# Writing the value projections and the fills of a context stage behind the small work of its pair

## The chip, the cores and the metric

The kernel runs on one NeuronCore of a Trainium2 chip. Its engines run side by side, each through its own queue in a fixed order: PE (TensorE) multiplies matrices, DVE (VectorE), ACT (ScalarE) and POOL (GpSimd) work on elements, and SP (SyncE) here only issues DMAs. The metric is the device time of one execution in microseconds. A profile of one execution gives each instruction's start and length; its times count from the start of the span.

## What is computed

Two layers of a backbone over 512 latent tokens and 256 context tokens, model width 1024, batch 1, all in float32. Layer 0, in which the change lies, is bidirectional RWKV-7 time mixing beside a gated short convolution; layer 1, a convolution module, isn't touched. What matters of layer 0:

```python
def wkv_scan(S0, r, decay, k, v, kk, a, reverse):
    def step(S, inp):
        r_t, w_t, k_t, v_t, kk_t, a_t = inp
        sa = jnp.einsum("bhvk,bhk->bhv", S, -kk_t)
        S = (S * w_t[:, :, None, :]
             + sa[..., None] * (kk_t * a_t)[:, :, None, :]
             + v_t[..., None] * k_t[:, :, None, :])
        return S, jnp.einsum("bhvk,bhk->bhv", S, r_t)
    ...
    rc, kc, vc, zac, bc, cc, xc, zbc = jnp.split(hc @ w_in, EVEN_SPLITS, axis=-1)
    yac, S_f, S_b = rwkv_seq(rwkv_prep(hc, rc, kc, vc, *rw), zero, zero, r_k, lnx_w, lnx_b, ctx_out)
    r, k, v, za, bg, cg, xb, zb = jnp.split(h @ w_in, EVEN_SPLITS, axis=-1)
    ya, _, _ = rwkv_seq(rwkv_prep(h, r, k, v, *rw), S_f, S_b, r_k, lnx_w, lnx_b, True)
    yb = bg * dwconv(cg * xb, sc_w, seg_len)
    y = jnp.concatenate([ya.astype(h.dtype) * jax.nn.silu(za), yb * jax.nn.silu(zb)], axis=-1) @ w_out
```

The scan runs over the context first, in both directions, and its end states start the scan over the latents. Of the context only these states are needed.

## The kernel before

The 16 heads lie in 8 pairs of 128 channels (0 to 7). The scan is done in chunks of 64 tokens: what happens within a chunk is matrix work that doesn't depend on the state ("small work"), and a "chain" carries the state from chunk to chunk. There are 12 stages. Stages 0 to 3 are context stages; one takes two head pairs together, with 4 chunks in each direction, and its state has a name c0 to c3. Stages 4 to 11 are latent stages l0 to l7, one head pair with 8 chunks each. So c2 holds the head pairs 4 and 5.

What a stage needs, and the helpers that write it:

- `project(p, which)` computes r, k or v (0, 1, 2) of head pair p: a weight block is loaded by SP in two halves (`wr`), ACT casts each to a high part (`wh`, L128), DVE subtracts the low part (`wl`, L129), and 24 matmuls (three products for each of 8 blocks of the contraction) go into `pl` for the 512 latent columns, for context stages 24 more into `pc` for 256 context columns. `shifted` mixes neighbouring tokens: one ACT pass (L370) and two DVE passes (L371, L373). The latent result goes to DRAM (`psp`) through POOL's queue.
- `prep_ctx(b)` projects k and v of both head pairs of a context stage. `prep_lat(p)` only loads k, v and r of a latent stage back.
- `fills(x)` holds the projections that a later stage needs: r of pair p when `FILL_R[p]` is x, and the gate z (`gate`, tile `pza`) when `FILL_Z[p]` is x. So `fills(1)` is z1 to z3, `fills(2)` r2, `fills(3)` r3 and z4 to z7, `fills(4)` r4 to r7. `conv_branch(p)` has four projections (`pcg`, `pxb`, `pbg`, `pzb`); branch 0 is written at the end of stage 3.
- `light` makes decays and scaled keys from k (tiles `ss`, `lw`, `la` on PE, then `AR`, `BK`). `heavy` does the products within chunks by a string of letters (`HEAVY`): V `pv`, the centred v copied into `UV` by four ACT copies (L640); B `pb`, transposes of keys into `BKt`; A `pa`, the products that are masked into `E` (in context stages `ectx`, L610); N copies of blocks of `E` into `Nt`; O the latent bonus.
- `solve` inverts small triangular blocks: a DVE transpose (L661) and 62 short DVE steps (L667, L669). `merge` completes the inverse (L675 to L694; its 64 matmuls go into `uh1`).
- `chain_ctx` and `chain_lat` are the chains (`zoc`, `zol`, `uh0`). A step goes PE, ACT, PE, ACT, PE, DVE; matmuls of the chains are pinned in the written order.

The main loop writes, in stage s, the chain of s, and then what the string `STAGE` says: O the bonus, F `fills(s + 1)`, P the preparation of stage s + 2, L and H light and heavy work of stage s + 2, S and M solve and merge of stage s + 1, C a conv branch. What is written earlier has the higher priority. A scheduler then fixes one order for each engine: it takes, by its own estimate of times, the ready instruction with the highest priority. So a letter's place in the string doesn't say where an instruction ends up, only what it yields to. The estimate ends there: on the chip each engine runs through its queue in that order.

Buffers also tie the parts: `k_`, `v_` and `Y` have one buffer each, `cg` and `yb` take turns for the latent results on their way to DRAM.

## Time and profile before

| | us |
|---|---|
| median of three runs | 1439.53 |
| lowest and highest of them | 1431.3, 1440.98 |
| the profiled execution | 1434.6 |
| its span, from the first to the last instruction | 1432.5 |

A line of a table of stretches gives the stretch, its length, the busy time of each engine with the number of instructions, and then the granted TensorE clock (1.00 is full speed), the busy share of the DMA engines and what they moved. PEld is the loading of weights into PE, beside its matmuls. A float32 matmul shows as two records, a transpose or one of the projections' as one. Matmuls are pipelined, and their ends are modelled, so that a PE which counts as busy isn't always at its peak. In the chain of work that ended last each row is a piece of time on the path to the end.

### The profile page before, as it was taken

Reading aid. Unit: us, or ns where it says so; the run is one execution under the profiler, and the core shown is the slowest. Engines: PE = TensorE matmul, PEld = TensorE weight load, DVE = VectorE, ACT = ScalarE, POOL = GpSimd, SP = SyncE. Lnnn points to the kernel's source line nnn. Section 1 sums busy time; section 2 is a strip of 40 time slices with the busy share of each in tenths; the row PEclk is TensorE's granted clock in tenths of the full one; section 3 lists DMA queues with packets and bytes.
Section 4 is the critical chain, followed back from the end, with each engine's and each line's share of the span. In section 5 each row is a group of like instructions: output and inputs, shape, how many; then the busy total and the mean of one; then the engine's idle time right before and its main releaser. Section 6 shows DMA issues by size and latency. Waiting matters only on the chain.

```text
span 1432.5 us, 29756 instructions
## 1 busy us (share of the span) xinstructions
PE 1376.7 (96%) x11921; PEld 1008.3 (70%) x11921; DVE 983.0 (69%) x2294; ACT 749.5 (52%) x1516; POOL 117.9 (8%) x246
## 2 busy tenths in 40 slices
PE   6899999999998998999999999999999999999998
PEld 1464677878776766666666666778777777788886
DVE  2675597568678989999999999656745545544333
ACT  4636355254555666756667565456753423464322
POOL 2023210000101101011010100010000000000000
PEclk9999999979898999999999999999999999999999
DMA  9754433222322221222222312358813303133322
GB/s 322 226 177 161 156 111 97 92 60 61 93 87 75 82 81 60 77 75 71 83 77 68 98 43 92 110 174 321 265 45 118 119 9 109 59 100 92 103 89 88
DMA packets 137626, 158.54 MB, mean 111 GB/s; under 512 B 15375, under 2 KB 104143, under 8 KB 137369
## 3 DMA queue, kind: packets, MB, share of 16 engines
q1 hardware_dynamic: 121104, 106.47, 23.7%
q0 software_dynamic: 15312, 48.99, 10.5%
q8 instruction: 94, 1.54, 0.4%
q10 hardware_dynamic: 1072, 1.19, 0.2%
q14 instruction: 44, 0.36, 0.1%
HBM read 138.33 MB, written 18.28 MB: 109 GB/s over the span
## 4 chain that ended last, share of the span: by engine, by line
PE 63%; DVE 14%; ACT 5%; issue 2%; DMA 0%; DVEq 0%; ACTq 0%
PE pu L57 12%; PE pz L57 6%; PE f L57 6%; PE o L57 5%; PE uh L57 4%; PE zol L57 4%; PE pcg L57 3%; PE pxb L57 3%; PE pza L57 3%; DVE E L610 2%; PE plk L57 2%; PE zoc L57 2%; PE pzb L57 2%; PE plv L57 1%; PE pac L57 1%
## 5 line engine op out<-in xcount | busy, mean ns | idle before, releaser
L57 PE MATMUL o<-wh,y 128*128 128x512 f32 x248 | 79.6, 397 | 0.0
L667 DVE TENSOR_TENSOR xtmpl<-Xl,Yl 128x126 f32<-128x126 f32 (+22 forms) x248 | 62.3, 251 | 2.8
L669 DVE TENSOR_TENSOR Yl<-Yl,xtmpl 128x126 f32<-128x126 f32 (+22 forms) x248 | 62.3, 251 | 2.7
L1152 ACT CAST ah<-a 64x512 fp32r<-64x512 f32 x32 | 19.8, 619 | 72.2 <-DVE a L1147 71.8
L57 PE MATMUL pal<-ARl,BKl 64*128 64x128 f32 x512 | 46.3, 300 | 10.7 <-DVE E L610 4.9
L57 PE MATMUL zol<-UV,E 64*64 64x64 f32 (+1 forms) x1024 | 54.2, 221 | 0.0
L57 PEld LDWEIGHTS o<-wh,y 128*128 128x128 f32 x248 | 45.9, 188 | 9.5
L57 PEld LDWEIGHTS pal<-ARl,BKl 64*128 64x128 f32 x512 | 36.4, 194 | 22.2 <-issue 7.2
L57 PE MATMUL zol<-Hl,ARl 64*64 64x64 f32 x896 | 50.2, 230 | 1.2 <-DVE Hl L782 1.0
L775 ACT COPY UV<-uh 64x128 f32<-64x128 f32 x128 | 33.2, 260 | 33.1 <-PE uh L57 25.6
L57 PE MATMUL o<-wl,y 128*128 128x512 f32 x124 | 49.4, 398 | 1.2 <-DVE wl L129 1.2
L57 PEld LDWEIGHTS zol<-Hl,ARl 64*64 64x64 f32 x896 | 35.0, 133 | 21.2 <-issue 17.0
L129 DVE TENSOR_TENSOR wl<-wr,wh 128x1024 fp32r<-128x1024 f32 x28 | 34.2, 1222 | 19.7 <-ACT wh L128 17.0
L57 PEld LDWEIGHTS uh<-UV,BKt 128*64 128x64 f32 x704 | 26.3, 137 | 28.7 <-ACT UV L775 23.0
L1147 DVE TENSOR_TENSOR a<-pu,a 128x512 f32<-128x512 f32 x16 | 11.0, 690 | 50.5 <-PE pu L57 48.2
L57 PEld LDWEIGHTS zol<-UV,E 64*64 64x64 f32 (+1 forms) x1024 | 42.4, 136 | 2.8 <-ACT UV L775 2.1
L610 DVE TENSOR_TENSOR E<-pal,maskE 128x512 f32<-128x512 f32 x64 | 42.9, 685 | 2.0 <-PE pal L57 1.2
L1107 DVE SCALAR_TENSOR_TENSOR pr<-px,dbe,What 119x512 f32<-119x512 f32 x32 | 22.6, 746 | 26.8 <-PE px L57 26.8
L782 DVE SCALAR_TENSOR_TENSOR Hl<-uh,PCl,HPl 128x64 f32<-128x64 f32 x112 | 26.5, 277 | 19.5 <-PE uh L57 8.6
L128 ACT CAST wh<-wr 128x1024 fp32r<-128x1024 f32 x28 | 29.6, 1056 | 19.7 <-DMA wr<-in_ev_w_out_dram 10.3
L886 POOL DMA_DIRECT2D mwr<-in_mod_w_dram x56 | 29.8, 537 | 112.8 <-PE uh L57 67.7
L57 PE MATMUL uh<-UV,BKt 128*64 128x64 f32 x704 | 36.3, 232 | 2.5 <-ACT UV L775 2.5
(947 smaller groups left out, 4230.9 us busy)
## 6 DMA issues: line engine op xcount, KB each, us to landing
mwr<-in_mod_w_dram POOLq DMA_DIRECT2D x56, 256.0 KB, 3.5
wr<-in_ev_w_out_dram SPq DMA_DIRECT2D x28, 512.0 KB, 5.1
ectx<-in_mod_w_dram SPq DMA_DIRECT2D x12, 512.0 KB, 5.2
wrk<-in_ev_w_in_dram SPq DMA_DIRECT2D x16, 256.0 KB, 3.1
wrv<-in_ev_w_in_dram SPq DMA_DIRECT2D x16, 256.0 KB, 4.1
wrr<-in_ev_w_in_dram SPq DMA_DIRECT2D x16, 256.0 KB, 2.7
wrza<-in_ev_w_in_dram SPq DMA_DIRECT2D x16, 256.0 KB, 2.8
wrcg<-in_ev_w_in_dram SPq DMA_DIRECT2D x16, 256.0 KB, 2.8
```

The costliest lines, as they stand in the source:

```text
L57: return T.matmul(o, lhsT, rhs, start=start, stop=stop)
L128: S.copy(hi, raw)
L129: env["lo"].tensor_tensor(out=lo, in0=raw, in1=hi, op=ALU.subtract)
L610: st["ev"].append(V.tensor_tensor(out=E[:, h, z * NLAT + c0 : z * NLAT + c0 + m, :], in0=pas[h], in1=maskE[:, z * (1 + h) : z * (1 + h) + ...
L667: V.tensor_tensor(out=tv, in0=X[:, :i, i : i + 1].to_broadcast([P, i, m]), in1=Y[:, i : i + 1, c0:].to_broadcast([P, i, m]), op=ALU.mult)
L669: V.tensor_tensor(out=Y[:, :i, c0:], in0=Y[:, :i, c0:], in1=tv, op=ALU.add)
L775: u_ = S.copy(UV[ZR[1 - h], i : 2 * nch - i : 2 * nch - 1 - 2 * i, ZR[h]], uh[ZR[1 - h], 0:2, :])
L782: h_ = V.scalar_tensor_tensor(out=Hn[:, z, :], in0=uh[:, 2 + z, :], scalar=PC[z][:, i : i + 1], in1=HP[:, z, :], op0=ALU.mult, op1=ALU.add)
L886: nc.gpsimd.dma_start(mws[q], I["mod_w"][layer, kt * P : (kt + 1) * P, c0 : c0 + 512])
L1107: V.scalar_tensor_tensor(out=pr[s][:NPROD], in0=px[s][:NPROD], scalar=dbe[:, 0:1], in1=What[:, n * 512 : n * 512 + 512], op0=ALU.add, op1= ...
L1147: V.tensor_tensor(out=a, in0=pp[1], in1=a, op=ALU.mult)
L1152: S.copy(ahl[s][hr], a[hr])
```

## The change

The string for the context stages is split in two. In stages 0 and 1 it becomes `KLSMHVvF`: K projects the keys of stage s + 2, then light, solve, merge and heavy work, then V projects the values, small v does `pv`, and the fills come last. In stages 2 and 3, where no values are projected, it becomes `OPLSMHF`: the fills stand last there too. The string of the latent stages stays. In `heavy` the context string loses V, and the O that did nothing there. `pv` and the bonus look up v when they run. For c0 and c1, ahead of the loop, k and v are still projected together, and `pv` is written behind `heavy`. The switch for a higher priority of weight splits (`env["first"]`) is False throughout.

```diff
-HEAVY = ("VBOAN", "ANBV")
-STAGE = ("OFPLSMH", "OSPLMHFC")
+HEAVY = ("BAN", "ANBV")
+STAGE = ("KLSMHVvF", "OPLSMHF", "OSPLMHFC")
...
-    env = {"lo": V}
+    env = {"lo": V, "first": False}
...
-        return hilo(src, raw, hi, lo)
+        with tc.high_priority() if env["first"] else nullcontext():
+            return hilo(src, raw, hi, lo)
...
-    def prep_ctx(b, between=None):
-        st = state(False, b)
-        for which in (1, 2):
+    def prep_ctx(b, between=None, st=None, kinds=(1, 2)):
+        st = st or state(False, b)
+        for which in kinds:
...
-        v_ = st["v"]
...
-            pv = ch3(ps_at(f"pv{nm}"))
+            pv, v_ = ch3(ps_at(f"pv{nm}")), st["v"]
...
-        st["po"] = po
+        st["po"], st["pv"] = po, pv
...
     heavy(sts[0])
+    sts[0]["pv"]()
...
     heavy(sts[1])
+    sts[1]["pv"]()
...
-        for x in STAGE[s >= 4]:
+        env["first"] = False
+        for x in STAGE[(s >= 2) + (s >= 4)]:
...
+            elif x == "K":
+                sts.append(prep_ctx(s + 2, kinds=(1,)))
+            elif x == "V":
+                prep_ctx(s + 2, st=sts[s + 2], kinds=(2,))
+            elif x == "v":
+                sts[s + 2]["pv"]()
...
-                sts.append(prep_ctx(s + 2) if s < 2 else prep_lat(s - 2))
+                sts.append(prep_lat(s - 2))
```

What the scheduler makes of it is seen at three places. Names carry the stage and a buffer number, and lines from 355 on have moved by one or more in the new file. First, ACT within the light work of c2, where the second half (`ac21`, `iPc21`) follows the first. Before:

```order
L527 ACTIVATE Pc20_2594<-Pc20_2594 128x528
L560 COPY BKc20_2607<-BKc20_2607 64x8x64
L529 COPY PCc20_2599<-Pc20_2594 128x8
L640 COPY UV000_1044<-pvc2_2786 64x8x64 x4
L520 ACTIVATE ac21_2621<-lac21_2618,hcol_77 128x256 x2
L526 ACTIVATE iPc21_2626<-Pc21_2624 128x512
```

Now:

```order
L528 ACTIVATE Pc20_2330<-Pc20_2330 128x528
L371 ACTIVATE vc2_2606<-pcv4_2619,omu_99 128x256
L530 COPY PCc20_2335<-Pc20_2330 128x8
L561 COPY BKc20_2343<-BKc20_2343 64x8x64
L128 CAST whv51_2684<-wrv51_2683 128x512
L521 ACTIVATE ac21_2357<-lac21_2354,hcol_77 128x256 x2
L527 ACTIVATE iPc21_2362<-Pc21_2360 128x512
```

The four copies of V have left this place; an evacuation of the value projection of pair 4 and a cast of the weights for pair 5 have come in.

Second, PE around `pv` of c2. Before, within the light work of c2 (`lac21`), between matmuls of the fill r2:

```order
L57 MATMUL lac21_2618<-lorc_488,lwc2h0_2549 128x256
L57 MATMUL plr2_3076<-hlh_117,whr20_3065 128x512
L57 MATMUL plr2_3076<-hll_118,whr20_3065 128x512
L57 MATMUL plr2_3076<-hlh_117,wlr20_3066 128x512
L57 MATMUL pvc2_2786<-ctr_106,vc2_2407 64x64 x16
L57 MATMUL plr2_3076<-hlh_117,whr20_3065 128x512
```

Now, behind the last mask products of c2 and 23 matmuls of the value projection of pair 5, with the fills z1 to z3 after it:

```order
L57 MATMUL plv5_2717<-hlh_117,whv51_2684 128x512
L57 MATMUL plv5_2717<-hll_118,whv51_2684 128x512
L57 MATMUL plv5_2717<-hlh_117,wlv51_2685 128x512
L57 MATMUL pvc2_2747<-ctr_106,vc2_2606 64x64 x16
L57 MATMUL pza1_2780<-hlh_117,whza10_2769 128x512
L57 MATMUL pza1_2780<-hll_118,whza10_2769 128x512
```

The values' projections now stand within the small work of c2, and the fills alone behind it, ahead of chain c1.

Third, PE at the first light matmuls of l0 (`ssl0`, `lwl00`). Before, behind the last fill z7 and ahead of chain c3:

```order
L57 MATMUL pza7_4081<-hll_118,whza71_4076 128x512
L57 MATMUL pza7_4081<-hlh_117,wlza71_4077 128x512
L57 MATMUL ssl0_4129<-sql0_4127,blk_105 128x512
L57 MATMUL lwl00_4150<-tanhl0_113,lwhl0_4123 128x512
L57 MATMUL lwl00_4150<-tanhl0_113,lwll0_4124 128x512
L57 MATMUL zoc3_0_4471<-UV010_1737,ectx_121 64x64 x8
L57 MATMUL plr4_4658<-hlh_117,whr40_4647 128x512
```

Now, inside chain c2, ahead of its second step:

```order
L57 MATMUL plr3_4276<-hlh_117,whr30_4265 128x512
L57 MATMUL plr3_4276<-hll_118,whr30_4265 128x512
L57 MATMUL ssl0_3923<-sql0_3921,blk_105 128x512
L57 MATMUL lwl00_3944<-tanhl0_113,lwhl0_3917 128x512
L57 MATMUL zoc2_1_3770<-Hc2_0_3731,ARc21_2372 64x64 x2
L57 MATMUL zoc2_1_3770<-Hc2_0_3731,ARc20_2342 64x64 x2
L57 MATMUL zoc2_1_3770<-Hc2_0_3731,ARc21_2372 64x64 x2
```

The light work of l0 has moved one chain ahead; z4 to z7, which stood before it, now stand behind it.

## The prediction

> **What bounds the kernel now.** I read the page first, then a table of stretches, then the chain of work that ended last. The page:

> ```profile
> span 1432.5 us, 29756 instructions
> PE 1376.7 (96%) x11921; PEld 1008.3 (70%) x11921; DVE 983.0 (69%) x2294; ACT 749.5 (52%) x1516; POOL 117.9 (8%) x246
> ...
> PE   6899999999998998999999999999999999999998
> ...
> DVE  2675597568678989999999999656745545544333
> ...
> PEclk9999999979898999999999999999999999999999
> ```

> PE is busy nearly everywhere, so time can only come out of stretches where it waits or runs at a lowered clock. The clock dips (slices 9, 11 and 13) all lie in the context stages. I cut these by the first matmul of each part (columns: stretch, length, then busy us of PE, PEld, DVE, ACT, POOL, then granted clock, DMA share, GB/s):

> ```profile
> core 0: us, PE busy (x) PEld busy (x) DVE busy (x) ACT busy (x) POOL busy (x), PEclk, DMA share, GB/s
> 191.90:225.90 34.00, 33.68 (x355) 24.57 (x355) 27.44 (x62) 22.49 (x44) 2.70 (x5) 1.00 0.32 95
> 225.90:253.30 27.40, 27.40 (x306) 20.48 (x307) 22.39 (x71) 13.83 (x35) 1.62 (x3) 1.00 0.27 82
> 253.30:287.00 33.70, 33.70 (x193) 29.68 (x193) 17.58 (x41) 10.15 (x18) 2.16 (x4) 1.00 0.30 95
> 287.00:320.90 33.90, 30.52 (x351) 24.26 (x350) 23.42 (x44) 19.89 (x40) 1.62 (x3) 0.79 0.21 63
> 320.90:346.10 25.20, 25.20 (x287) 19.89 (x286) 19.07 (x62) 13.82 (x35) 0.55 (x1) 0.95 0.15 44
> 346.10:363.30 17.20, 17.16 (x98) 14.91 (x97) 12.79 (x39) 4.62 (x8) 1.08 (x2) 1.00 0.28 86
> 363.30:396.20 32.90, 30.99 (x349) 23.31 (x347) 24.15 (x45) 20.53 (x41) 5.66 (x10) 0.83 0.31 90
> 396.20:425.00 28.80, 28.80 (x288) 21.75 (x289) 22.62 (x70) 15.78 (x39) 1.62 (x3) 0.96 0.28 80
> 425.00:457.00 32.00, 27.21 (x263) 20.53 (x263) 30.17 (x71) 16.74 (x29) 5.66 (x10) 0.83 0.31 98
> 457.00:484.10 27.10, 26.13 (x348) 19.19 (x345) 21.48 (x66) 18.66 (x45) 1.20 (x3) 0.95 0.20 62
> 484.10:520.50 36.40, 34.01 (x315) 26.15 (x313) 35.20 (x82) 21.88 (x37) 4.59 (x8) 1.00 0.31 91
> 520.50:919.50 399.00, 381.37 (x5315) 269.43 (x5315) 361.19 (x1053) 250.92 (x601) 38.95 (x70) 1.00 0.24 71
> ```

> From the top: small work of pair c1; chain c0; keys and values of c2 alone; small work of c2; chain c1; values of c3 alone; small work of c3; chain c2; small work of latent pair l0; chain c3; small work of l1 with conv branch 0; the latent stages. The waiting is in the small work of c2, c3 and l0 (clock 0.79, 0.83, 0.83), while 33.7 and 17.2 us go to projections that cover nothing. The chain that ended last, in the projections and in the small work of c2 (start, length, what):

> ```profile
> 261.88 2.88 PE pck L57 x24
> 264.75 5.56 PE plk L57 x24
> ...
> 287.23 0.86 PE ssc L57 x2
> ...
> 296.58 0.48 ACT UV L640
> 297.08 0.58 ACT UV L640
> 297.67 0.58 ACT UV L640
> 298.26 0.58 ACT UV L640
> 298.87 0.84 ACT ac L520 x2
> ...
> 301.28 0.69 DVE ARc L551
> ...
> 306.67 1.92 PE uh L57 x64
> 308.58 3.61 PE pac L57 x32
> ...
> 316.31 3.60 PE pac L57 x30
> ```

> The path goes through the four copies of V (L640), which stand on ACT ahead of the second half of the light work, and then through `pac`, 3.60 us for 30 records. In the small work of c1 the same 30 take 2.00 us (timeline rows; the second is pv):

> ```profile
> 219.49 2.00 PE L57 MATMUL pac<-ARc,BKc 64*128 64x64 f32 x30
> ...
> 294.35 1.15 PE L57 MATMUL pvc<-ctr,vc 64*64 64x64 f32 x32
> ```

> **Prices.** A projection is 24 matmuls: 5.56 us over the latent columns, 2.88 over the context ones. So k or v of a context pair is 16.9, a fill 5.56, conv branch 0 22.2. Taking off each stretch the projections that the order puts in it leaves the rest:

> - a chain: c0 27.4 - 16.7 (z1 to z3) = 10.7; c1 25.2 - 14.6 (k7 and nearly all of k6) = 10.6; c2 28.8 - 18.3 (79 matmuls of z4 to z7) = 10.5. I use 10.6.
> - small work: c1 34.0 - 15.5 (67 matmuls) = 18.5; c2 33.9 - 7.9 (r2, 19 context matmuls of k6) = 26.0; c3 32.9 - 9.5 (r3, 17 of z4) = 23.4; l0 32.0 - 12.0 (r4, r5, 4 of r6) = 20.0; l1 36.4 - 22.2 = 14.2.

> So c2 waits some 7.5 us, c3 5, l0 6; all that cover could win is about 18 us. Other prices, groups of the context stages:

> ```profile
> L640 ACT COPY UV<-pvc 64x512 f32<-64x512 f32 x4 | 2.3, 580 | 0.0
> ...
> L128 ACT CAST whk<-wrk 128x512 fp32r<-128x512 f32 x3 | 1.9, 623 | 2.1 <-PE plv L57 2.1
> ...
> L520 ACT ACTIVATE ac<-lac,hcol 128x256 f32<-128x256 f32 x4 | 1.7, 470 | 0.6 <-PE lwc L57 0.6
> ...
> L669 DVE TENSOR_TENSOR Yc<-Yc,xtmpc 128x126 f32<-128x126 f32 (+22 forms) x93 | 23.7, 254 | 2.4
> ...
> L610 DVE TENSOR_TENSOR E<-pal,maskE 128x512 f32<-128x512 f32 x16 | 10.6, 684 | 1.2 <-PE pal L57 1.2
> ...
> L373 DVE SCALAR_TENSOR_TENSOR lr<-plr,hmu,lr 128x511 f32<-128x511 f32 x6 | 4.4, 741 | 0.1
> ...
> wrv<-in_ev_w_in_dram SPq DMA_DIRECT2D x16, 256.0 KB, 4.1
> ```

> **The change, part by part.** No arithmetic is added or removed; every term is an instruction that stands elsewhere. From the end of the small work of c1 (225.9) to the first latent chain (520.5) the kernel takes 294.6 us now. In the new order:

> 1. Chain c0 is covered by k4, k5 in place of z1 to z3: 10.7 + 16.9 = 27.6.
> 2. Small work of c2 holds v4, v5 up to the first matmul of the last one (11.6 us of projections, not 7.9). On the path, the copies of V go (-2.3), but the first evacuation of v (a 128x256 pass of ACT, as L520's: 0.47) and one cast (0.62) come in: -1.2. The extra shifts on DVE fall into its waits (23.4 busy of 33.9). 33.9 - 1.2 = 32.7. Bounds: 18.5 + 11.6 = 30.1 if it runs as c1's did, 26.0 + 11.6 = 37.6 if the larger cover only adds.
> 3. Behind it, uncovered: the other 23 matmuls (5.3), pv (1.15), z1 to z3 (16.7): 23.1. DVE meanwhile solves c2.
> 4. Chain c1 with k6, k7: 27.5.
> 5. Small work of c3: 32.9 - 1.2 = 31.7 (30.1 to 35.0).
> 6. Uncovered: 5.3 + 1.15 + r2 5.56 = 12.0.
> 7. Chain c2 with the light work of l0 inside it, the rest of l0, merge of c3, r3 and z4 to z7. PE: 10.6 + 16.0 (14.2 as in l1, second transpose and pv 1.8) + 27.8 = 54.4. DVE: 22.6 + 30.2 now, 26 solve steps of c3 fewer (-6.6), 34 of l0 more (+8.6), one evacuation pair fewer (-1.5), two masks and a bonus more (+2.1): 55.4. Neither fits beside the other without loss; the latent stages, with the same mix, run DVE at 361.2 of 399.0 (0.905): 55.4 / 0.905 = 61.2. Bounds: 55.4, and one after the other 10.6 + 20.0 + 4.1 (what l0's stretch now leaves to the next: masks' matmuls, transposes, pv) + 27.8 = 62.5.
> 8. Chain c3, l1, r4 to r7, conv branch 0. PE 10.6 + 1.0 + 16.0 + 44.4 = 72.0, of which the last 26.4 us are projections alone; the 45.6 before at the latent stages' PE share (381.4 of 399.0): 47.7. 74.1 (72.0 to 76).

> Sum 289.9, 4.7 less than now. One transpose and pv of l1 (1.8) now stand after 520.5 and are done earlier in the new order: -6.5. The latent stages' own strings are unchanged, so I cost them at nothing; the cover there is the same work in nearly the same order.

> Queues: the weight loads move with their projections on SP. The second half of v5 is loaded behind the two stores of the chain's state, as that of k5 is now; it has 18 us until PE wants it, against 4.1 for a load and 1.3 for cast and difference. On POOL the spills of v stand behind the load of the unit matrix, which waits for the merge; their buffers are written next 20 us later. Both cost nothing, hidden by that work; if the cover failed, 4.1 each.

> The profiled execution took 1434.6 us (span 1432.5); the three runs beside it have the median 1439.5, 0.3% above. Against its own time: 1434.6 - 6.5 = **1428 us**. Why so little: DVE and PE are near full together from 396 on, and the new order leaves 22.0, 10.9 and 26.4 us of projections that cover nothing (parts 3, 6, 8), where now 33.7 and 17.2 stand.

> **Rivals.**

> B, the cover brings the clock back. For it: c1's small work, with 15.5 us of projections in it, shows 1.00 and `pac` at 2.00. Against it: in the new order merge and `pac` still follow each other with six projection matmuls between, as now. Every low bound at once: 27.6 + 30.1 + 23.1 + 27.5 + 30.1 + 12.0 + 55.4 + 72.0 = 277.8, so 294.6 - 277.8 + 1.8 = 18.6 less: 1416 us. [...]

> C, DVE's queue becomes the bound: it is in order, and the values' shifts and the pulled-in solve steps now stand between the light work, the masks and the chain's state updates. For it: 35.2 of 36.4 in l1's stretch. Against it: 23.4 of 33.9 in c2's. Every high bound: 27.6 + 37.6 + 23.1 + 27.5 + 35.0 + 12.0 + 62.5 + 76 = 301.3, 6.7 - 1.8 more: 1439.5, slower than now. It decides from DVE shares above 0.9 in the small work of c2 and c3 on.

> That the change does nothing is excluded by the order: the three places shown all differ.

> **How the numbers follow.** Forecast 0.55, B 0.23, C 0.22. The range goes from B's end, less 2, to C's end plus 6.5 (the span from this execution to the slowest of the runs): 1414 to 1446. About 1% is what a measurement of this kernel tells from no change. Faster by more (below 1420): B's 0.23 and 0.04 of the forecast, 0.27. Slower by more (above 1449): 0.09, the part of C in which the latent stages inherit the delay. Within: 0.64.

> **What would show it.** Each step has its stretch: the small work of c2 and c3 near 32.7 and 31.7 us with L640 gone from the chain; granted clock there still near 0.8 (1.00 with 2.00 us for `pac` would be B); the first light matmul of l0 inside chain c2; DVE above 0.9 from there to chain c3 and idle beside conv branch 0; the first latent chain some 5 us earlier. Wrong would be: PE waiting for projections' casts inside the chains, or DVE above 0.9 in c2's small work (C).

## The result, and the profile after

| | before | after |
|---|---|---|
| median of 6 runs, us | 1438.55 (1431.3 to 1440.98) | 1424.16 (1421.41 to 1426.41) |
| ratio, 95% interval | | 0.991 (0.9892 to 0.9927) |
| the profiled execution, us | 1434.6 | 1423.9 |
| its span, us | 1432.5 | 1421.6 |
| PE busy in it, us | 1376.7 | 1366.3 |
| rest of the span (PE not busy), us | 55.8 | 55.3 |

The forecast was 1428, so the time is 4 us below it and the sign is right. The forecast took 6.5 us off the execution of 1434.6; the spans of the two profiled executions differ by 10.9 us, and the means of all runs (in the table of the experiments) by 12.5. The reason is mostly another one. From the page of the changed kernel:

```profile
span 1421.6 us, 29736 instructions
...
PE 1366.3 (96%) x11921; PEld 999.9 (70%) x11921; DVE 981.5 (69%) x2294; ACT 748.4 (53%) x1516; POOL 118.0 (8%) x246
...
PE   6999998999989998999999999999999999999998
...
PEclk9999998999999999999999999999999999999999
```

PE runs the same 11921 matmuls, and it waits as long as before (55.3 us against 55.8). What became shorter is the matmuls themselves: 10.4 of the 10.9 us of the span are PE's busy time. PE has 23.9 us less of half clock (below), and a microsecond of that costs 0.37 to 0.44 us by the runs further down, which makes 9 to 10.5 us: they come from the clock. The stretches of the changed kernel, cut as in the prediction (same columns; the first row is the small work of c1, then follow the parts 1 to 8 of the prediction, last the latent stages):

```profile
194.30:229.10 34.80, 32.73 (x314) 24.49 (x312) 24.64 (x52) 18.87 (x38) 2.71 (x5) 0.95 0.30 92
229.10:263.00 33.90, 32.20 (x372) 25.64 (x372) 26.27 (x83) 17.69 (x43) 1.09 (x2) 0.90 0.15 46
263.00:289.50 26.50, 25.40 (x320) 20.36 (x319) 24.79 (x57) 18.28 (x37) 1.62 (x3) 1.00 0.24 73
289.50:312.60 23.10, 23.10 (x129) 18.68 (x131) 19.99 (x55) 10.94 (x18) 1.62 (x3) 1.00 0.35 107
312.60:341.10 28.50, 27.83 (x333) 22.58 (x334) 14.60 (x49) 12.90 (x35) 1.08 (x2) 1.00 0.22 65
341.10:367.60 26.50, 25.46 (x321) 20.43 (x320) 23.93 (x47) 18.31 (x37) 5.15 (x9) 1.00 0.28 86
367.60:379.70 12.10, 12.10 (x81) 9.60 (x81) 9.68 (x25) 7.41 (x13) 1.08 (x2) 1.00 0.33 100
379.70:438.00 58.30, 53.39 (x649) 40.57 (x650) 55.84 (x155) 36.74 (x76) 6.79 (x12) 1.00 0.30 90
438.00:509.70 71.70, 69.33 (x700) 53.36 (x694) 55.17 (x126) 42.50 (x87) 7.41 (x14) 1.00 0.34 100
509.70:909.90 400.20, 384.06 (x5286) 270.86 (x5286) 360.84 (x1053) 245.27 (x593) 38.97 (x70) 0.99 0.24 71
```

The small work of c2 and of c3 takes 26.5 us at clock 1.00, where it took 33.9 at 0.79 and 32.9 at 0.83. On the other side, chain c0 (33.9 against 27.4 before) became longer, at 0.90, and the small work of c1 a little (34.8 against 34.0): places where the prediction saw no harm. What lies ahead of c1 ended at 194.3 instead of 191.9; over all profiles of this study that moment lies between 191.9 and 198.7, whatever the kernel.

The profile records when the granted clock changes. In these records it is either full or half (1.00 or 0.50), and each stretch of half clock lasts one to five times 3.41 us (3.4 to 17.1 us in the rows below). Cut along those records, before (ahead of the first, one window of full clock; then the small work of c2, of c3, of l0):

```profile
302.90:306.30 3.40, 1.22 (x18) 0.87 (x18) 3.40 (x6) 3.07 (x6) 0.54 (x1) 1.00 0.00 0
306.30:323.40 17.10, 16.73 (x221) 15.40 (x222) 7.15 (x12) 4.96 (x10) 0.54 (x1) 0.50 0.21 63
384.80:398.50 13.70, 13.70 (x145) 11.59 (x144) 5.72 (x9) 3.45 (x8) 0.55 (x1) 0.50 0.26 79
446.30:459.90 13.60, 13.14 (x184) 10.06 (x183) 9.67 (x16) 4.54 (x9) 1.63 (x3) 0.50 0.30 98
```

With one window of 3.4 us at the start (50.3 us), that is 47.8 us of half clock. (A last stretch, which runs into the end of the span, is left out here and below.) After, all of it (the start; c1; chain c0; the first latent stage):

```profile
48.00:54.80 6.80, 6.16 (x24) 5.50 (x25) 6.70 (x20) 6.80 (x13) 0.00 (x0) 0.50 0.95 292
225.50:232.30 6.80, 6.80 (x81) 6.03 (x80) 1.98 (x3) 2.37 (x4) 0.00 (x0) 0.50 0.08 25
239.10:242.50 3.40, 3.40 (x26) 2.42 (x26) 3.06 (x14) 1.35 (x5) 0.48 (x1) 0.50 0.20 77
549.70:556.60 6.90, 6.56 (x40) 5.09 (x41) 6.54 (x28) 2.58 (x5) 0.00 (x0) 0.51 0.27 78
```

23.9 us, so half of it went: the long stretches in c2, c3 and l0 are gone, and new short ones came in c1, in chain c0 and later. The full clock between two of these stretches also lasts whole multiples of 3.41 us: before, 61.4 us from 323.4 to 384.8 and 47.8 from 398.5 to 446.3 (18 and 14 times), after, 6.8 from 232.3 to 239.1 and 307.2 from 242.5 to 549.7 (2 and 90 times).

### The profile page after: what moved, and what is told of

It is laid out like the page before. It is cut to its first block, busy times and chain, and to the rows that moved or that the text cites. A ratio compares the mean times of both kernels' runs of the same rounds, so it can differ in the third digit from the quotient of the medians.

```text
span 1421.6 us, 29736 instructions
## 1 busy us (share of the span) xinstructions
PE 1366.3 (96%) x11921; PEld 999.9 (70%) x11921; DVE 981.5 (69%) x2294; ACT 748.4 (53%) x1516; POOL 118.0 (8%) x246
## 3 DMA queue, kind: packets, MB, share of 16 engines
q0 software_dynamic: 15312, 48.99, 10.8%
## 4 chain that ended last, share of the span: by engine, by line
PE 67%; DVE 16%; ACT 7%; issue 5%; DMA 4%; POOL 0%; DVEq 0%; SPq 0%; ACTq 0%; POOLq 0%
PE pu L57 13%; PE pz L57 6%; PE f L57 6%; PE uh L57 5%; PE zol L57 4%; PE pcg L57 4%; PE o L57 3%; PE pxb L57 3%; PE plk L57 3%; PE plr L57 2%; DVE E L610 2%; PE plv L57 2%; PE pzb L57 1%; PE zoc L57 1%; PE pac L57 1%
## 5 line engine op out<-in xcount | busy, mean ns | idle before, releaser
L57 PE MATMUL o<-wh,y 128*128 128x512 f32 x248 | 79.7, 397 | 0.0
L667 DVE TENSOR_TENSOR xtmpl<-Xl,Yl 128x126 f32<-128x126 f32 (+22 forms) x248 | 62.6, 252 | 3.1
L669 DVE TENSOR_TENSOR Yl<-Yl,xtmpl 128x126 f32<-128x126 f32 (+22 forms) x248 | 62.3, 251 | 2.9
L57 PE MATMUL zol<-UV,E 64*64 64x64 f32 (+1 forms) x1024 | 54.0, 221 | 0.0
L57 PEld LDWEIGHTS o<-wh,y 128*128 128x128 f32 x248 | 45.9, 188 | 9.5
L57 PE MATMUL o<-wl,y 128*128 128x512 f32 x124 | 49.6, 400 | 1.9 <-DVE wl L129 1.8
L57 PE MATMUL zol<-Hl,ARl 64*64 64x64 f32 x896 | 50.2, 230 | 1.1 <-DVE Hl L782 0.6
L57 PE MATMUL pal<-ARl,BKl 64*128 64x128 f32 x512 | 45.0, 296 | 6.4 <-DVE E L610 5.6
L775 ACT COPY UV<-uh 64x128 f32<-64x128 f32 x128 | 33.3, 260 | 32.8 <-PE uh L57 26.6
L57 PEld LDWEIGHTS zol<-Hl,ARl 64*64 64x64 f32 x896 | 35.0, 133 | 21.3 <-issue 17.3
L57 PEld LDWEIGHTS uh<-UV,BKt 128*64 128x64 f32 x704 | 26.3, 137 | 30.9 <-ACT UV L775 24.5
L57 PEld LDWEIGHTS pal<-ARl,BKl 64*128 64x128 f32 x512 | 35.5, 191 | 16.7 <-DVE E L610 5.5
L57 PEld LDWEIGHTS zol<-UV,E 64*64 64x64 f32 (+1 forms) x1024 | 42.3, 136 | 2.5 <-ACT UV L775 2.0
L610 DVE TENSOR_TENSOR E<-pal,maskE 128x512 f32<-128x512 f32 x64 | 43.2, 686 | 0.6 <-PE pal L57 0.3
L1117 DVE SCALAR_TENSOR_TENSOR pr<-px,dbe,What 119x512 f32<-119x512 f32 x32 | 22.6, 746 | 26.9 <-PE px L57 26.8
L128 ACT CAST wh<-wr 128x1024 fp32r<-128x1024 f32 x28 | 29.6, 1056 | 20.4 <-PE o L57 13.6
L57 PE MATMUL uh<-UV,BKt 128*64 128x64 f32 x704 | 36.3, 232 | 3.8 <-ACT UV L775 2.4
L782 DVE SCALAR_TENSOR_TENSOR Hl<-uh,PCl,HPl 128x64 f32<-128x64 f32 x112 | 26.4, 278 | 17.4 <-PE uh L57 8.0
## 6 DMA issues: line engine op xcount, KB each, us to landing
mwr<-in_mod_w_dram POOLq DMA_DIRECT2D x56, 256.0 KB, 3.9
wrk<-in_ev_w_in_dram SPq DMA_DIRECT2D x16, 256.0 KB, 2.8
wrv<-in_ev_w_in_dram SPq DMA_DIRECT2D x16, 256.0 KB, 5.0
wrr<-in_ev_w_in_dram SPq DMA_DIRECT2D x16, 256.0 KB, 2.8
wrza<-in_ev_w_in_dram SPq DMA_DIRECT2D x16, 256.0 KB, 2.8
wrcg<-in_ev_w_in_dram SPq DMA_DIRECT2D x16, 256.0 KB, 2.8
```

Source lines behind the costliest of these rows:

```text
L57: return T.matmul(o, lhsT, rhs, start=start, stop=stop)
L128: S.copy(hi, raw)
L610: st["ev"].append(V.tensor_tensor(out=E[:, h, z * NLAT + c0 : z * NLAT + c0 + m, :], in0=pas[h], in1=maskE[:, z * (1 + h) : z * (1 + h) + ...
L667: V.tensor_tensor(out=tv, in0=X[:, :i, i : i + 1].to_broadcast([P, i, m]), in1=Y[:, i : i + 1, c0:].to_broadcast([P, i, m]), op=ALU.mult)
L669: V.tensor_tensor(out=Y[:, :i, c0:], in0=Y[:, :i, c0:], in1=tv, op=ALU.add)
L775: u_ = S.copy(UV[ZR[1 - h], i : 2 * nch - i : 2 * nch - 1 - 2 * i, ZR[h]], uh[ZR[1 - h], 0:2, :])
```

## The experiments

Two theories stood against each other for the gain. "Copies": as the forecast had it, the four copies of V left ACT's path and the rest is overlap. "Cover" (rival B): the value projections, now inside the small work, hold the clock up. And two for the loss in c1 and chain c0: the copies of V of c1, now between the small work and the first step of the chain, or the weights of k4, which come late. The last columns give the profiled execution (half clock counted as above) and the mean of the granted clocks of all its kernel's runs. The ratios of e1 to e4, of e5 to e9 and of e10 to e13 are each to runs of the kernel before on the same chip, whose medians differ by 2 us between the three.

| run | median, us | ratio to before, 95% | span | PE busy | half clock, us | mean clock of the runs |
|---|---|---|---|---|---|---|
| before (58 runs, mean 1436.7) | 1436.4 to 1438.5 | 1 | 1432.5 | 1376.7 | 47.8 | 0.9818 |
| after | 1424.16 | 0.991 (0.9892 to 0.9927) | 1421.6 | 1366.3 | 23.9 | 0.9918 |
| e1 pv of c0, c1 back | 1417.95 | 0.9865 (0.9842 to 0.9887) | 1420.7 | 1366.6 | 27.3 | 0.9933 |
| e2 pv behind, nothing else | 1430.27 | 0.9961 (0.9947 to 0.9974) | 1430.7 | 1373.5 | 44.4 | 0.9844 |
| e3 fills first | 1429.95 | 0.9953 (0.9936 to 0.997) | 1427.7 | 1365.1 | 27.3 | 0.9880 |
| e4 late fills first | 1428.72 | 0.9948 (0.9926 to 0.9969) | 1430.1 | 1373.8 | 44.4 | 0.9879 |
| e5 dense work added to before | 1437.65 | 1.0006 (0.9987 to 1.0025) | 1436.3 | 1381.7 | 47.8 | 0.9829 |
| e7 values between the halves of pac | 1422.94 | 0.9914 (0.9889 to 0.9938) | 1423.5 | 1366.6 | 20.5 | 0.9925 |
| e8 values ahead of the heavy work | 1428.69 | 0.995 (0.9932 to 0.9969) | 1427.4 | 1367.0 | 23.9 | 0.9915 |
| e9 fills first, pv back | 1424.8 | 0.9924 (0.9897 to 0.9952) | 1426.3 | 1371.3 | 37.5 | 0.9886 |
| e10 the changed kernel again | 1422.29 | 0.9895 (0.9871 to 0.9919) | 1418.0 | 1363.4 | 17.1 | 0.9922 |
| e11 e1 again | 1418.39 | 0.9864 (0.9836 to 0.9893) | 1419.3 | 1367.0 | 27.3 | 0.9927 |
| e12 dense work in c2 | 1423.61 | 0.9897 (0.987 to 0.9924) | 1419.8 | 1366.9 | 20.5 | 0.9923 |
| e13 values between, c2 alone | 1418.5 | 0.9859 (0.983 to 0.9887) | 1417.5 | 1363.1 | 20.5 | 0.9930 |

The runs of one kernel differ in their clock, and their times go with it. Inside e4, for one, they go from 1424.22 us at a mean clock of 0.992 to 1434.52 at 0.983. Fitted within each of the 13 rows below the first (103 runs), 0.001 of mean clock is 1.06 us (correlation 0.81). A clock lower by 0.001 over some 1425 us is 2.85 us of half clock, so a microsecond of half clock costs about 0.4.

### pv of c0 and c1 back (e1), alone and with the fills first (e3, e9)

e1, on the changed kernel:

```diff
-        for x in HEAVY[lat]:
+        for x in ("" if an or lat else "V") + HEAVY[lat]:
...
-    sts[0]["pv"]()
...
-    sts[1]["pv"]()
```

> The changed kernel, but pv of c0 and c1 stands again ahead of the transposes of the heavy work (as before); c2 and c3 stay changed. Open is why the small work of c1 and chain c0 together take 71.1 us in the changed kernel (191.9 to 263.0) where 61.4 stood before and 61.6 were forecast. Theory 'copies': the four copies of V of c1 now stand on ACT between Nt and the chain's first copies (232.95 to 235.32 on the chain of waits, then lr 0.69), so with pv back they leave the path: 71.1 becomes 68.0 to 68.7 and the median falls by 2.4 to 3 us against the changed kernel, to about 0.988 to 0.989 of before. Theory 'late weights': the loss comes from the weights of k4, which land 5.24 us on the chain of waits (217.09 to 222.36) and leave PE without dense work, whatever pv does: 71.1 stays within 1 us, 0.990 of before.

The 71.1 and 61.4 of this expectation were cut at different points. From the first matmul of r0 to the end of the covering projections it is 62.6 us before (190.9 to 253.5), 69.6 in the changed kernel (193.2 to 262.8) and 62.4 in e1 (193.2 to 255.6): 7.2 us won in place, and 6 in the median. It beats both kernels. That is more than the copies alone (2.4 to 3). The chain of waits of the changed kernel shows where the rest comes from:

```profile
217.09 5.24 DMA wrk<-in_ev_w_in_dram
...
222.41 0.63 ACT whk L128
...
223.06 0.69 DVE wlk L129
223.76 0.61 DVE ectx L610
...
225.51 3.60 PE pac L57 x30
...
232.31 0.61 ACT Nt L629
...
232.95 0.58 ACT UV L640
...
234.74 0.58 ACT UV L640
...
235.34 0.69 ACT lr L371
...
236.34 0.70 PE zoc L57 x16
```

Two things are to be seen. The mask (L610) stands in DVE's queue behind the split of a weight of k4, which waits for its load; PE waits for the mask (2.0 us), and then the 30 of `pac` take 3.60 us at half clock. And behind `pac` the four copies of V and one of r1 stand between Nt and the first step of chain c0. In e1 the split waits for the same load and ends at the same time (223.7), but more of r1 stands ahead of that half of `pac` in PE's order, so PE works through the wait, no half clock follows, and the first step of chain c0 ends its sum at 229.8 instead of 237.0. Here the half clock goes with the order in every profile: 6.8 us set in between 224.6 and 231.0 in the four that have pv of c1 behind its heavy work (the changed kernel, e3, e4, e10), and none at this place in the ten others. So the late weights are in both kernels; they cost only where nothing covers them. The first theory was right about the edit, and short by the half clock that goes with it.

e3 and e9 are the changed kernel and e1 with the fills of the first two stages ahead of the keys:

```diff
-STAGE = ("KLSMHVvF", "OPLSMHF", "OSPLMHFC")
+STAGE = ("FKLSMHVv", "OPLSMHF", "OSPLMHFC")
```

> The changed kernel with the fills (z1 to z3, r2) of the first two stages ahead of the keys again, as before; values and pv stay behind. Theory 'late weights': chain c0 is again covered by z1 to z3, whose weights were there in time before, so the small work of c1 and chain c0 return from 71.1 to 61.4 to 64 us and up to 9 us are won: 0.984 to 0.986. Theory 'copies' (pv of c1 on ACT): 71.1 falls by no more than 1, 0.990. Both expect the small work of c2 and c3 at clock 1.00 with pac at 2.0, since the values still cover them: 26 to 28 us each. If the clock falls to 0.8 there, the cover came from the place of the fills and not from the values.

> The changed kernel with pv of c0 and c1 back ahead, and the fills of the first two stages ahead of the keys as before (what the third run did, without the loss in c1). It tells what the place of the fills z1 to z3 and r2 is worth by itself. If it is worth something (DVE solves c2 beside z1 to z3, and chain c1 then waits for less): 4 to 6 us slower than with the fills last, 1422 to 1424, 0.990. If the place of these fills is worth nothing and the loss of the third run came from half clock elsewhere: 1418, 0.9865.

The small work of c2 in e3 shows full clock, as both theories had it, and c1 with chain c0 takes 66.3 us (197.7 to 264.0), 3.3 less than in the changed kernel, where "late weights" wanted up to 9 and "copies" 1: both are in it. But the whole is 6 us slower than the changed kernel. With pv back (e9), c1 and chain c0 are at 62.5 (192.1 to 254.6), and the whole 7 slower than e1. So the four runs form a square: by the medians pv back is worth 5 to 6 us with the fills in either place, the fills last 6 to 7 with pv in either place (by the ratios to the kernel before 4 to 6 and 6 to 8). Between e9 and e1 the mean clock differs by 0.0047, by the fit 5.0 us: the place of the fills works mostly through the clock as well. The 1418 of the expectation for e9, by which the place is worth nothing, is refuted; that the loss is mostly half clock fits the clocks. In e9's profile 10.2 us of it stand in c2 and 20.5 between 406 and 492 us.

### Copies alone (e2)

On the kernel before; fills first and k and v together, as there:

```diff
-        for x in HEAVY[lat]:
+        for x in HEAVY[lat] if an is None or lat else "BAN":
...
                 heavy(sts[s + 2], st)
+                if s < 2:
+                    sts[s + 2]["pv"]()
```

> The kernel before, with pv of c2 and c3 alone moved behind the heavy work (k and v projected together and fills first, as before). Theory 'copies of V' (the forecast's): the four copies (2.3 us) leave ACT ahead of the second half of the light work in c2 and in c3: each small work 2 us shorter, about 1434 us, 0.997, clock in c2 still near 0.8. Theory 'cover' (rival B): what made the small work of c2 and c3 6 to 7 us shorter than forecast is the value projections inside it, which hold the clock at 1.00 and let 30 of pac take 2.0 us; without them the clock stays at 0.79 and 0.83, pac at 3.60, the small work stays at 32 to 34 us, 0.997 to 1.000. If the small work here shows clock 1.00 and 27 us, the cover theory falls.

6 us faster than before: rather more than the forecast's 4.6 for the copies in both pairs, and more than "cover" allowed. But the half clock stayed where it was, in c2 and in c3:

```profile
306.10:323.20 17.10, 16.49 (x252) 14.84 (x254) 8.70 (x15) 5.39 (x10) 1.08 (x2) 0.50 0.14 48
384.70:398.30 13.60, 13.60 (x156) 11.12 (x154) 5.33 (x7) 4.78 (x9) 0.54 (x1) 0.50 0.20 62
```

So what e2 moves is one part of the gain (of 5.9 us between the means, 2.8 go with the clock by the fit and 3.1 remain). It is not the copies alone: in e2 the scheduler also put the first light matmuls of c3 ahead of its values (at 349.4). In c2, where PE's order stays nearly the same, the first light matmul to the last of `pac` takes 31.8 us against 32.8 before, 1.0 less and not 2.3. And what freed c2 and c3 of half clock is not pv's place. That leaves the values inside the small work; e3, with the fills first and full clock in both, shows that the fills behind them aren't needed for it.

### The late fills (e4)

The changed kernel with stages 2 and 3 as before:

```diff
-STAGE = ("KLSMHVvF", "OPLSMHF", "OSPLMHFC")
+STAGE = ("KLSMHVvF", "OFPLSMH", "OSPLMHFC")
```

> The changed kernel with the fills of stages 2 and 3 (r3, z4 to z7; r4 to r7) ahead of the small work again, as before. Theory 'fills' (steps 7 and 8 of the forecast): PE then waits in the small work of l0 again (clock 0.83, 6 us of waiting beyond its 26 us of work), 5 to 6 us slower than the changed kernel, 0.994. Theory 'values': all that the change wins comes from the values in the small work of c2 and c3, and the late fills only move time about: within 1.5 us of the changed kernel, 0.989 to 0.991.

5 us slower than the changed kernel, as "fills" had it, and the half clock of l0 is back. But c2 also shows half clock, though the order on every engine is the changed kernel's up to chain c2. First e4 (c2 from the first light matmul to the end of pv; l0), then the changed kernel (c2):

```profile
262.60:300.30 37.70, 36.56 (x376) 29.64 (x374) 30.62 (x69) 22.72 (x44) 1.62 (x3) 0.86 0.21 63
441.90:455.50 13.60, 12.98 (x183) 10.51 (x183) 9.09 (x15) 4.07 (x8) 1.08 (x2) 0.50 0.27 78
```

```profile
262.80:296.00 33.20, 32.10 (x376) 25.74 (x374) 29.40 (x65) 22.78 (x44) 1.62 (x3) 1.00 0.21 64
```

The same 376 matmuls in the same order take 4.5 us longer with 10.2 us of half clock, 0.44 for each. What precedes the half clock in e4 and in e1's c2 (each the window of 3.4 us ahead, and then the half clock):

```profile
281.50:284.90 3.40, 3.08 (x97) 2.84 (x96) 3.16 (x7) 2.85 (x6) 0.55 (x2) 1.00 0.33 82
284.90:295.10 10.20, 10.20 (x112) 8.86 (x111) 4.62 (x8) 2.75 (x5) 0.29 (x1) 0.50 0.16 54
```

```profile
274.90:278.30 3.40, 3.40 (x102) 3.04 (x100) 3.32 (x6) 2.44 (x5) 1.08 (x2) 1.00 0.55 139
278.30:292.00 13.70, 13.70 (x122) 11.49 (x123) 5.84 (x9) 4.23 (x7) 0.00 (x0) 0.50 0.07 26
```

PE is busy in all of 274.9 to 278.3. But its 102 matmuls are `pac`, `uh` and `zoc`, of 64x64 and 32x32, and not one is a projection. So in e1 half clock set in behind small matmuls alone, without any wait of PE. They don't always bring it: in the changed kernel the window from 283.5 on, with `pac` and `uh` alone (110 matmuls, PE busy for 3.40 of 3.40 us), was followed by full clock.

### Dense work added (e5, e12)

On the kernel before in c2 and c3 (e5), and on e1 in c2 alone (e12: `nm == "c2"` in place of `an and not lat`), matmuls of 128 rows whose output the next matmuls of `pac` overwrite:

```diff
                     for c in range(m):
+                        for h in (1, 0) if an and not lat and c in (0, 2, 4) else ():
+                            go(pas[h].rearrange("p c x -> p (c x)")[:, c * x :], hlat[0][:, 0, 0:P], hlat[0][:, 0, c * x : 512])
                         for h in (1, 0):
```

> The kernel before, with twelve dense matmuls (128 rows, 512, 384 or 256 columns) added to pac of c2 and twelve to pac of c3; each writes columns of pac's bank that the pair's own matmuls overwrite, so nothing is computed otherwise. By the projections' rate (512 columns in 0.22 us) they add 1.95 us of PE work to each pair, 3.9 us in all. Theory 'clock': c2 and c3 lose time because PE, though busy, does only small matmuls (32x32 and 64x64) for several us, and the granted clock halves; dense matmuls among them keep it at 1.00. The records of before show half clock for 17.1 us in c2 and 13.7 us in c3; without them the mean clock rises from 0.982 to about 0.992, worth 11 to 12 us by the spread of the run before this (1424.2 us at 0.992 to 1434.5 us at 0.983 for one and the same kernel). Net 7 to 9 us faster than before though work is added: 0.994 to 0.995. Theory 'order' (the clock follows from what PE waits for, and the gain of the change is what left the path): added work costs what it costs, 1.003, and the clock in c2 and c3 stays at 0.8.

> The kernel of the first run with the twelve dense matmuls of the fifth in pac of c2 alone. There they came behind the window that started the half clock; here, in the order of PE, two of them stand among the first eight of zoc and the rest in every stretch of pac and on both sides of uh. They add 1.95 us. Theory 'clock': no run has half clock in c2 (13.7 us in one profile of the kernel without them, none in its fastest runs), so the mean clock is 0.994 to 0.996 in nearly all runs, the spread shrinks and the added work is won back: 1416 to 1419 us, 0.986 to 0.988, and c2's small work about 32 + 2 us in the profile. Theory 'order': clocks as without them (0.990 to 0.996), and 2 us slower, 1420, 0.988; half clock may stand in the profile of c2 in spite of them.

e5 gave neither number: 1.0006. In c2 the half clock lasted 17.1 us again, since it had begun at 307.2 and the first added matmul came with `pac` at 310.6; in c3 it was gone, but 13.6 us stood at other places further on, and the mean clock did not rise by what was expected. It decides nothing. e12 put the matmuls ahead of the place. In its profile c2 has no half clock, and c2 up to the end of z3 is 2.3 us shorter than in e11, although the added work makes some 2 us (1.95 in the expectation, 2.1 at the projections' 5.56 us for 24 matmuls of 512 columns; e11's rows: c2 to z3, chain c2 to z7; then e12's):

```profile
254.50:310.70 56.20, 55.31 (x461) 44.59 (x461) 45.11 (x117) 30.08 (x57) 3.25 (x6) 0.88 0.27 80
377.70:435.20 57.50, 52.58 (x630) 39.89 (x629) 55.12 (x153) 36.02 (x75) 6.81 (x12) 1.00 0.31 91
```

```profile
255.60:309.50 53.90, 53.04 (x475) 41.79 (x475) 45.81 (x120) 29.84 (x56) 3.24 (x6) 1.00 0.27 81
376.80:437.40 60.60, 55.51 (x634) 42.26 (x632) 56.04 (x155) 36.07 (x76) 6.79 (x12) 0.94 0.30 86
```

Here a stretch with more work was faster at full clock: the clock is a cause there, and not a sign of waiting. That the added work is what held the clock is less sure, since it is one execution against two (e1, e11). The total missed, though. The median is 5 us above e11's, and the mean clock no higher; in the profile half clock appeared in l0 instead (0.94).

### Values elsewhere (e7, e8, e13), and repeats (e10, e11)

On e1, the values between the two halves of `pac` (e7 in c2 and c3, e13 in c2 alone), or ahead of the heavy work (e8):

```diff
             for gi, (z, g) in enumerate(PA_ORDER if lat else ((0, 0), (1, 0))):
+                if gi == 1 and mid:
+                    mid()
...
-                heavy(sts[s + 2], st)
+                heavy(sts[s + 2], st, (lambda: prep_ctx(s + 2, st=sts[s + 2], kinds=(2,))) if s < 2 else None)
```

```diff
-STAGE = ("KLSMHVvF", "OPLSMHF", "OSPLMHFC")
+STAGE = ("KLSMVHvF", "OPLSMHF", "OSPLMHFC")
```

> The changed kernel with pv of c0 and c1 back ahead (1418 us before this run, 0.9865), and the values of c2 and c3 written between the two halves of pac instead of behind the heavy work; in the order of PE 19 (c2) and 24 (c3) projection matmuls now stand ahead of the second half of pac, where 64 of uh and 32 of pac followed each other nearly without one. Theory 'clock': the half clock of c2 (13.7 us in one profile of the kernel compared with) goes or shrinks to under 7 us; in c3 64 of uh and 16 of pac still follow each other, so a short dip is still possible. Mean clock about 0.995 in most runs, 1415 to 1416 us, 0.985. Theory 'order': the same work in another order, clock as before, 1418, 0.9865 or slower since masks and solve of c2 start some 4 us later.

> As the run with the values between the halves of pac, but the values are written ahead of the whole heavy work (pv still behind it), so that pac falls among the fills z1 to z3 and r2: no more than 32 of uh or 17 of pac follow each other without a projection's matmul. Theory 'clock': no half clock in c2 or c3 in any run, mean clock 0.995 to 0.996, 1414 to 1416 us, 0.984 to 0.985. Theory 'order': masks, Nt, pv and the solve of c2 come later than there, at the end of the covering work: 1420 us or more, 0.988.

> The kernel of the first run with the values between the two halves of pac in c2 alone (the seventh run had it in c2 and c3: there c2 became 6 us shorter, and c3 and the later stages gave it back with another order). With c3 written as before, PE's order from chain c1 on is the first run's. If what c2 wins stays won: 1413 to 1416 us, 0.983 to 0.986, mean clock 0.994 or more. If it is given back at the next wait (DVE's queue in l0 and l1): 1418, 0.9865.

e7 and e13 did in c2 what was expected: no half clock in the profile, and c2 up to the end of z3 in 50.3 us in e13 against 56.2. But e7 ended 5 us slower than e1 (in its profile 6.8 us of half clock stand in c3, at 356.0), and e13 just as fast as e11 on the same chip. In e13 the profile shows where it went (c2 to z3; chain c2 to z7):

```profile
254.30:304.60 50.30, 49.45 (x461) 39.50 (x459) 42.86 (x108) 29.89 (x56) 3.25 (x6) 1.00 0.29 88
371.60:433.70 62.10, 57.10 (x632) 43.40 (x630) 56.06 (x155) 36.06 (x76) 6.80 (x12) 0.92 0.29 84
```

From within chain c1 on, e13's instructions stand in e11's order on every engine. Still its chain c2 and l0 take 62.1 us with 10.2 of half clock, where e11 takes 57.5 without. Neither gain nor loss is bound to the written order alone. e8 missed "clock": its profile has 3.4 us of half clock in c2 and in c3, and 23.9 in all, as much as the changed kernel's. It is 10 us slower than e1. Of the 6.7 us between the two spans PE's time outside its busy time makes 6.3 (60.4 against 54.1), so PE waits more for what came later; its longest waits between c2 and the latent stages:

```profile
PE uh L57 <- DVE amc L676: 3.0, 2, 1.8
PE uh L57 <- ACT UV L721: 2.5, 2, 2.2
```

In e11 these are 1.6 and 0.7.

> The changed kernel once more, on the chip of the next three. In the profile of it c2's small work shows clock 1.00; in the profile of the fourth run, whose PE order is the same up to chain c2, it shows 10.2 us of half clock there, and pv of c2 starts 36.5 us after the first light matmul instead of 32.1. If half clock is a matter of when the small matmuls fall against a fixed grid of 3.41 us, this kernel too has runs with and without it: mean clocks from 0.989 to 0.993 and times that go with them, about 1.1 us for each 0.001, median 1424, 0.991. If half clock is set by the order of the instructions, all runs show the clock of the first profile, 0.991 to 0.993, and the 10.2 us above came from the changed later stages.

> The kernel of the first run once more (pv of c0 and c1 ahead again), beside the changed kernel on one chip. Both theories: 1418, 0.9865; the difference from the changed kernel is 6 us, of which 2.4 to 3.1 for the copies of V that leave ACT's queue and 4 for 10.2 us of half clock in c1 and chain c0 (0.4 us lost for each us, as c2 shows: 4.4 us for 10.2). If the difference shrinks below 3 us, the part of the clock was chance.

e10 has 0.991 to 0.993 in all runs, and its profile the same 6.8 us of half clock in c1 and none in c2: in the changed kernel these places are steadier than the first theory had it, and e4's half clock in c2 did not come up. That is what the second theory expected; but e4's order first differs some 100 us behind that half clock, so its later stages don't explain it, and neither theory holds as it stands. e11 repeats e1. The difference between the means of both pairs of runs is 5.2 us (1423.5 and 1418.2), and the clocks differ by 0.001 only, so 4 of it are order: e1 gains the half clock of c1, but shows 13.7 us in c2 in both its profiles.

Over all profiles c2 and c3 differ in this. In c3 all nine that have the values ahead of `pac` there as in the change (the changed kernel, e1, e3, e4, e9 to e13) run at full clock and take 26.6 us from the first light matmul to the last of `pac`; before it was 31.8, with half clock from 384.8 on. In c2 seven have the values in that place and nothing added. Three run at full clock, in 26.6 or 26.7 us (the changed kernel, e3, e10), and four have 10.2 or 13.7 us of half clock and take 29.7 to 31.9 (e1, e4, e9, e11), against 17.1 us and 32.8 before. So with the values there the clock is full in c3 each time, and in c2 only sometimes.

## Why the prediction was right where it was, and wrong

| step | forecast, us | measured, us |
|---|---|---|
| up to c1 (no step) | 191.9, unchanged | 194.3 |
| small work of c1 (no step) | 34.0, unchanged | 34.8 |
| 1 chain c0 | 27.6 | 33.9 |
| 2 small work of c2 | 32.7 | 26.5 |
| 3 behind it | 23.1 | 23.1 |
| 4 chain c1 | 27.5 | 28.5 |
| 5 small work of c3 | 31.7 | 26.5 |
| 6 behind it | 12.0 | 12.1 |
| 7 chain c2 and l0 | 61.2 | 58.3 |
| 8 chain c3, l1, conv branch 0 | 74.1 | 71.7 |
| 1 to 8 | 289.9 | 280.6 |

All rows together, the first latent chain starts 10.8 us earlier, which is nearly the whole difference of the spans; behind it the sum is nothing (911.9 us to the end, 912.0 before). The 1.8 us of l1 don't show there. They may have been won and lost again: the first latent stage has 6.8 us of half clock (549.7) that the kernel before doesn't have, some 3 us by the price above. No run separates the two.

- Steps 3, 4 and 6, the projections that cover nothing, were right to 1 us: counts of matmuls by a measured rate.
- Steps 2 and 5 failed on their choice of clock. "The granted clock there still near 0.8" did not come true: 1.00, and `pac` in 2.00 us, which the prediction had named as the sign of B:

```profile
287.48 2.00 PE L57 MATMUL pac<-ARc,BKc 64*128 64x64 f32 x30
```

  The reason against B was that merge and `pac` still follow each other with few projections between. It looked at the small matmuls and not at the window ahead of them. Before, the half clock of c2 followed 3.4 us in which PE was busy for 1.22; with the values there, PE was busy for 3.07, 3.40 and 3.40 us in the three windows from 280.1 on, around `pac`, and no half clock followed. The reason wasn't empty, though: in e1 a window of small matmuls alone was followed by half clock in c2. Both steps even went below their lower bound (30.1), it seems because that took c1's small work as the floor (18.5 us beside its projections), which has pv (1.15) and its copies (2.3) in it; 26.5 - 11.6 = 14.9 is that without them.
- That the copies of V leave the path came true, but their price (2.3 us in each pair) isn't shown: e2 wins some 3 us for both beyond what goes with the clock, and 1.0 in place in c2.
- Step 1 was mis-sized by 6.3 us, and what is done to c1 wasn't a step at all. The edits to the first two pairs were read as changing c2 and c3 only; pv of c1 behind its heavy work puts the copies ahead of chain c0, on the same queue. e1 shows this: 7.2 us in place, 5.2 between the means.
- Step 7 was inside its bounds and its mechanism right: DVE 55.84 busy of 58.30. Step 8 ended 0.3 below its bound. With the fills behind the small work l0 kept full clock in both profiles of the changed kernel and both of e1, and e4, without them there, shows 13.6 us of half clock again. They don't secure it: e12 and e13, with the fills in the same place, have 6.8 and 10.2 us there.
- Rival B was the mechanism in c3, and in c2 in both profiles of the changed kernel, and its 1416 was missed by about what step 1 lost. e1, with that undone, stands at 1418, though with half clock in c2. Rival C did not come: DVE is at 24.79 of 26.50 (0.94) in c2's small work, above the 0.9 from which it was to decide, and PE hardly waits for it.

By the fit, the clock (0.9818 to 0.9918 in the means) makes 10.6 of the 12.5 us between the means of the runs. In steps 2 and 5 the forecast had 11.4 us too much, in c1 and step 1 7.1 too little. That these two errors partly cancel is luck, and so is how close the number came.

Open: what decides, between two executions with the same order, whether half clock sets in, as in c2 of the changed kernel and of e4; why e12 is 5 us slower than e11 and not 2; and whether an order exists that keeps the clock up in c2, c3 and l0 at once. No version tried beats e1 by more than the interval.

## What to carry to other kernels

Take PE's busy time and its waits apart before explaining a gain: here the waits stayed and the same matmuls became shorter, by what the lower half clock accounts for. In this kernel 3.4 us of small matmuls alone were followed by half clock in e1's c2 and by full clock in the changed kernel's. Where large ones stood around them, written so that they are still there when the small ones become ready, c3 had full clock in nine profiles of nine and c2 in three of seven. What is saved in one such place can be lost in the next, so look at the clock of the whole kernel, over several runs, and not at the stretch alone. When a step is moved for some of the iterations, work out its new neighbours on each queue for every iteration that gets it, the first ones too.
